# Larger DMA packets on both rings of a sliding-window copy: 32 KB in place of 16 KB

## The chip, the core and the metric

The kernel runs on one core of a Trainium2 chip. The metric is the device time of one execution in microseconds. A profile of one execution is also taken: it records every instruction and every DMA packet.

## What is computed

The input `x` has 32 batches of 4096 rows of 256 float32 numbers. The output holds 127 overlapping windows of 64 rows for each batch, one every 32 rows:

```python
for i in range(n_windows):            # 127
    start = i * stride                # stride 32
    result[:, i] = x[:, start:start + window_size]   # window_size 64
```

Nothing is calculated; it is a copy. Cut each batch into 128 blocks of 32 rows (32 KB each). Window w is block w followed by block w + 1, so every block but the first and the last of a batch is written twice. The input has 134 MB, the output 266 MB.

## The kernel before

The kernel consists of DMAs alone. There are two ways to make the windows, and each has a DMA queue of its own.

**Direct** (queue of SP, `Direct.windows`, line 45; the profile calls this queue q1): the first 21 batches are copied from HBM to HBM. One DMA moves 16 windows of 64 KB. As 127 is not a multiple of 16, the last DMA of a batch moves 15 windows; it is called the *tail* below. This path reads nearly every input block twice.

**Staged** (queue of ACT, `Staged`; q10 in the profile): the last 11 batches go through SBUF. A load (`Staged.load`, line 79) brings 16 blocks, one to each of 16 partitions of a slot. Two stores (`Staged.store`, line 91) write them out, once as the first half of a window and once as the second half. At the edges of a batch a store has 15 blocks. There are 24 slots (`N_TILES` = 6 tiles of four). The order on ACT is written out by hand in `Staged.run`: ten loads ahead (`LEAD`), then in each turn the load of group r + 10 and the two stores of group r. A store waits for the semaphore `loaded` of its slot. A load that reuses a slot waits for the semaphore `stored`, which the two earlier stores raise.

SP and ACT each feed one ring on each of the 16 DMA engines. Each window or block of a DMA goes to one engine. `max_dma_last_dim` sets how long a contiguous piece may be, in bytes, before it is cut. In the kernel before it is 16384 for the full direct DMAs (`DIRECT`) and for loads and stores (`STAGE`), and 32768 for the tail (`2 * DIRECT`). A full direct DMA therefore gives each engine four packets of 16 KB, a tail two packets of 32 KB, and a load or a store two packets of 16 KB. Each DMA ends with a 4-byte packet on every engine that it uses, which raises the semaphore; this is called the completion.

At the end SP waits until the semaphore `done` has counted all direct DMAs and the last stores.

Of the kernel before, what the change touches and what calls it, by code (L numbers as in the profile page):

```python
# [1 line left out]

# [4 lines left out]


DIRECT, STAGE = 16384, 16384
N_STAGED = 11  # L10
N_TILES = 6
LEAD = 10


class Geometry:


    def __init__(self, tc, x, out, B, L, D, W, S, n_win):
        assert W == 2 * S and L % S == 0 and n_win == L // S - 1
        self.x, self.out = x, out  # L20
        self.blk, self.nb, self.nw = S * D, L // S, n_win
        self.done, self.total = tc.alloc_semaphore("done"), 0

    def xap(self, b, block, dims):
        return bass.AP(self.x.tensor, self.x.offset + (b * self.nb + block) * self.blk, dims)

    def oap(self, b, w, half, dims):
        at = ((b * self.nw + w) * 2 + half) * self.blk
        return bass.AP(self.out.tensor, self.out.offset + at, dims)

    def count(self, dma):
        dma.then_inc(self.done, 16)
        self.total += 16


class Direct:


    def __init__(self, g, batches):
        self.g, self.batches = g, batches  # L40

    def windows(self, q, b, w0, n, size):
        g = self.g
        g.count(
            q.dma_start(
                out=g.oap(b, w0, 0, [[2 * g.blk, n], [1, 2 * g.blk]]),
                in_=g.xap(b, w0, [[g.blk, n], [1, 2 * g.blk]]),
                max_dma_last_dim=size,
            )
        )  # L50

    def run(self, q):
        full = self.g.nw // 16 * 16
        for b in self.batches:
            for w0 in range(0, full, 16):
                self.windows(q, b, w0, 16, DIRECT)
            self.windows(q, b, full, self.g.nw - full, 2 * DIRECT)


class Staged:  # L60

    def __init__(self, g, tc, pool, dtype, batches, n_tiles):
        self.g = g
        tiles = [pool.tile([128, g.blk], dtype, name=f"xb{i}") for i in range(n_tiles)]
        self.slots = [t[32 + c : 96 : 4, :] for t in tiles for c in range(4)]
        self.loaded = [tc.alloc_semaphore(f"loaded{i}") for i in range(len(self.slots))]  # L70
        self.stored = [tc.alloc_semaphore(f"stored{i}") for i in range(len(self.slots))]
        self.groups = [(b, j) for b in batches for j in range(0, g.nb, 16)]

    def load(self, q, r):
        g, (b, j) = self.g, self.groups[r]
        n, i = divmod(r, len(self.slots))
        if n:
            q.wait_ge(self.stored[i], 32 * n)
        q.dma_start(
            out=self.slots[i], in_=g.xap(b, j, [[g.blk, 16], [1, g.blk]]),  # L80
            max_dma_last_dim=STAGE,
        ).then_inc(self.loaded[i], 16)

    def store(self, q, r):
        g, (b, j) = self.g, self.groups[r]
        n, i = divmod(r, len(self.slots))
        q.wait_ge(self.loaded[i], 16 * (n + 1))
        for half in (0, 1):
            lo = 1 if half and j == 0 else 0
            hi = 15 if not half and j + 16 == g.nb else 16  # L90
            dma = q.dma_start(
                out=g.oap(b, j + lo - half, half, [[2 * g.blk, hi - lo], [1, g.blk]]),
                in_=self.slots[i][lo:hi, :],
                max_dma_last_dim=STAGE,
            )
            if r + len(self.slots) < len(self.groups):
                dma.then_inc(self.stored[i], 16)
            else:
                g.count(dma)

    def run(self, q, lead):
        for r in range(lead):
            self.load(q, r)
        for r in range(len(self.groups)):
            if r + lead < len(self.groups):
                self.load(q, r + lead)
            self.store(q, r)


@with_exitstack  # L110
def kernel(
    ctx: ExitStack,
    tc: tile.TileContext,
    x: bass.AP,
    window_size: bass.AP,
    stride: bass.AP,
    out: bass.AP,
):
    nc = tc.nc
    W, S = int(window_size), int(stride)  # L120
    B, L, D = x.shape
    n_win = (L - W) // S + 1
    assert out.shape == (B, n_win, W, D)
    g = Geometry(tc, x, out, B, L, D, W, S, n_win)
    pool = ctx.enter_context(tc.tile_pool(name="xb", bufs=1))
    staged = Staged(g, tc, pool, x.dtype, range(B - N_STAGED, B), N_TILES)
    direct = Direct(g, range(B - N_STAGED))
    with tc.tile_critical():
        staged.run(nc.scalar, LEAD)
        direct.run(nc.sync)  # L130
        nc.sync.wait_ge(g.done, g.total)


# [1 line left out]
_INS = ['x', 'window_size', 'stride']  # L135
_OUTS = [((32, 127, 64, 256), 'float32')]

_NUMBERS = {'window_size': 64, 'stride': 32}


# [26 lines left out]
```

## Time and profile before

| | |
|---|---|
| median of 6 runs | 759.18 us (755.99 to 762.4) |
| the profiled execution | 755.99 us; span from its first to its last instruction 754.2 us |
| DMA traffic | 25314 packets, 312.53 MB; 6869 of them are completions |
| direct (q1) | 12705 packets, 174.80 MB, 55.4% of the 16 engines' time |
| staged (q10) | 12606 packets, 137.71 MB, 43.8% |
| DMAs | 147 full direct, 21 tails, 88 loads, 176 stores |

The page gives the DMA engines' share of time in 40 equal slices of the span, as tenths, and below that the GB/s of each slice. The bytes are counted once for each packet. A direct packet costs HBM a read and a write, a load one read, a store one write. The queue lines give packets, MB and the share of the time of the 16 engines that the packets took. The issue lines give the kind of DMA, how many there were, their size, and the median time from issue to landing. A table by time can be asked for any stretch of the span; its last column is again GB/s. A share slightly over 1 arises because a packet's recorded end overlaps the start of the next one by a few nanoseconds.

### The profile page before, as it was taken

What the parts mean: (1) busy time and instruction counts of PE and PEld (TensorE: products, weight loads), DVE (VectorE), ACT (ScalarE), POOL (GpSimd) and SP (SyncE); (2) the same over time, 40 slices, a digit from 0 to 9 for tenths busy, and PEclk for the clock granted to TensorE, in tenths of its full rate; (3) what the DMA queues carried; (4) which work ended last, traced back from release to release, by engine and by line L of the source; (5) the groups of instructions that cost most, each with busy time, mean ns of one, the idle gap of its engine ahead of it and who ended that gap; (6) DMA issues with size and microseconds to landing.
All of it is one profiled execution on the core that took longest, in us unless ns stands there. A gap on an engine that the chain in (4) does not pass through costs nothing. (4 is left out here: it accounts for less than half of the span.)

```text
span 754.2 us, 482 instructions
## 1 busy us (share of the span) xinstructions
POOL 0.2 (0%) x4
## 2 busy tenths in 40 slices
POOL 0000000000000000000000000000000000000000
DMA  8999999999999999999999999999999999999996
GB/s 359 421 403 413 418 424 422 416 423 416 427 418 418 424 420 419 428 415 428 423 425 419 426 421 421 425 418 421 422 423 420 424 419 428 416 424 408 404 403 271
DMA packets 25314, 312.53 MB, mean 414 GB/s; under 512 B 6869, under 2 KB 6869, under 8 KB 6869
## 3 DMA queue, kind: packets, MB, share of 16 engines
q1 hardware_dynamic: 12705, 174.80, 55.4%
q10 hardware_dynamic: 12606, 137.71, 43.8%
q14 instruction: 3, 0.02, 0.0%
HBM read 220.92 MB, written 266.34 MB: 646 GB/s over the span
## 5 line engine op out<-in xcount | busy, mean ns | idle before, releaser
L148 POOL MEMSET const-bfloat16-1.0<- 128x1 bf16 x1 | 0.1, 101 | 0.0
L148 POOL MEMSET const-uint8-127<- 128x1 uint8 x1 | 0.1, 101 | 0.0
L148 POOL MEMSET const-float32-0.0<- 128x1 f32 x1 | 0.1, 98 | 0.2 <-issue 0.2
L148 POOL MEMSET const-float32-1.0<- 128x1 f32 x1 | 0.1, 98 | 0.0
## 6 DMA issues: line engine op xcount, KB each, us to landing
out_dram<-in_x_dram SPq DMA_DIRECT2D x147, 1024.0 KB, 70.0
out_dram<-xb ACTq DMA_DIRECT2D x154, 512.0 KB, 68.8
xb<-in_x_dram ACTq DMA_DIRECT2D x88, 512.0 KB, 71.7
out_dram<-in_x_dram SPq DMA_DIRECT2D x21, 960.0 KB, 69.1
out_dram<-xb ACTq DMA_DIRECT2D x22, 480.0 KB, 69.4
```

The source lines that it names most:

```text
L148: nc = _bacc.Bacc("TRN2", target_bir_lowering=False, num_devices=1)
```

## The change

`DIRECT` and `STAGE` become 32768, and the tail's size becomes `DIRECT`, so that it stays at 32768 bytes:

```diff
-DIRECT, STAGE = 16384, 16384
+DIRECT, STAGE = 32768, 32768
...
-            self.windows(q, b, full, self.g.nw - full, 2 * DIRECT)
+            self.windows(q, b, full, self.g.nw - full, DIRECT)
```

Every data packet of the kernel is then 32 KB: two for each engine in a direct DMA, one in a load or a store. The number of DMAs, their order, their queues, their semaphores and their completions stay as they were.

## The prediction

> **What bounds the kernel now.** No compute engine works here, so I read the DMA lines of the page first: how busy the 16 DMA engines are, what each queue carried, and how long a DMA takes from issue to landing.
>
> ```profile
> span 754.2 us, 482 instructions
> DMA  8999999999999999999999999999999999999996
> GB/s 359 421 403 413 418 424 422 416 423 416 427 418 418 424 420 419 428 415 428 423 425 419 426 421 421 425 418 421 422 423 420 424 419 428 416 424 408 404 403 271
> DMA packets 25314, 312.53 MB, mean 414 GB/s; under 512 B 6869, under 2 KB 6869, under 8 KB 6869
> q1 hardware_dynamic: 12705, 174.80, 55.4%
> q10 hardware_dynamic: 12606, 137.71, 43.8%
> out_dram<-in_x_dram SPq DMA_DIRECT2D x147, 1024.0 KB, 70.0
> out_dram<-xb ACTq DMA_DIRECT2D x154, 512.0 KB, 68.8
> ```
>
> The engines are busy 99.2% of the span (55.4 + 43.8). A DMA lands some 70 us after its issue, so each ring holds tens of microseconds of work in reserve and a late issue costs nothing. The bytes don't change. What can change the time is how fast one engine gets through its packets.
>
> Next, the stretches near the end, as a table by time (columns: length, POOL, clock, DMA share, GB/s):
>
> ```profile
> 100.00:690.00 590.00, 0.00 (x0) 1.00 1.01 421
> 690.00:740.00 50.00, 0.00 (x0) 1.00 0.95 404
> ```
>
> After 690 us the share is 0.95, about 15/16: one engine has finished. The 21 direct tails (15 windows) and 22 of the stores (15 blocks) run on 15 engines. The completion records agree: the 12705 packets of q1 are 147 x 64 + 21 x 30 data packets and 147 x 16 + 21 x 15 completions. So 15 engines set the end. Each carries 588 direct and 528 staged packets of 16 KB, 42 direct ones of 32 KB and 432 completions.
>
> Durations come from the trace's packet records. The usual 16384 B packet lasts 611 ns and the next on its engine starts 607 ns after it; the usual 32768 B packet lasts 1213 ns, period 1209; a completion takes 6 ns of its engine. Hence 602 ns per 16 KB and 5 ns per packet. One engine: 1116 x 607 + 42 x 1209 + 432 x 6 ns = 730.8 us. The first packet starts at 2.4 us of the span and the last ends at about 752, so some 19 us on the slowest engine are neither bytes nor fixed cost. They are **stretch**: packets that last longer than 611 or 1213. Following packets end to start, I find 13 to 21 us of it per engine (about 16) and only 1 to 5 us of gaps. So the stretch is the only thing of size that this change can act on.
>
> From 60 to 682 us the records show:
> - 16 KB direct packets: mean stretch 12.1 ns (12% of them over 15 ns)
> - 16 KB staged packets: 12.2 ns (12%)
> - 32 KB packets (the tails): 51.3 ns (38%)
>
> Two 16 KB packets carry 24.3 ns, one 32 KB packet 51.3. After 682 us it is under 1 ns for every kind.
>
> The table by time shows the same without the records. First four windows in which a tail is moving, then four beside them:
>
> ```profile
> 212.70:221.80 9.10, 0.00 (x0) 1.00 1.01 414
> 353.80:366.00 12.20, 0.00 (x0) 1.00 1.00 412
> 389.70:401.40 11.70, 0.00 (x0) 1.00 1.00 413
> 425.00:437.10 12.10, 0.00 (x0) 1.00 1.00 416
> ...
> 228.00:246.00 18.00, 0.00 (x0) 1.00 1.01 421
> 334.00:352.00 18.00, 0.00 (x0) 1.00 1.01 428
> 369.00:387.00 18.00, 0.00 (x0) 1.00 1.01 430
> 405.00:423.00 18.00, 0.00 (x0) 1.00 1.02 431
> ```
>
> Over all 17 tails between 70 and 650 us the mean is 415 GB/s, over 16 windows beside them 425. The tails already have the packet size that the change gives to all.
>
> [...] and completions count as turns. This is the queue view of the tail window 353.8 to 366:
>
> ```profile
> q1 hardware_dynamic: 192, 2.93, 58.1%
> q10 hardware_dynamic: 192, 2.10, 42.2%
> ```
>
> 192 packets each. [...]
>
> **The change part by part.** The instruction lists differ only in shapes: 16x4x4096 becomes 16x2x8192 for the 147 full direct DMAs, 16x2x4096 becomes 16x8192 for the 88 loads and 176 stores; tails keep 15x2x8192. No DMA, wait or queue order is added or moved.
>
> 1. Fixed cost: an engine's 1116 packets of 16 KB become 558 of 32 KB; 558 x 5 ns = **-2.8 us**, all on the path.
>
> 2. Stretch: the 558 pairs cost 558 x 24.3 = 13.6 us now (average over the loaded part). At the 32 KB rate they cost 558 x 51.3 = 28.6. About 95% lie before the loads end, so **+14 us**. Its bounds are wide. Below: if the tail's stretch belongs to the tail, or to mixing two sizes, it is 0. It may even fall: if stretch goes with the number of descriptors, 1158 data and 432 completions become 600 and 432, and 16 us become 10. Above: 16 KB packets suffer too while 32 KB ones run. Stretch summed over all engines is 259 ns per us with none in flight, 529 with 2 to 4 engines on one, 616 with 4 to 6, 750 with 6 to 8. A line through the ends, carried to 16 engines, gives some 1380, 8.6% of engine time against 2.1% now: +44 us over 670 us. I take the packets' own rate, as 16 engines on 32 KB have not been seen, nor 32 KB on the SBUF side at all.
>
> 3. Turns: per engine before, direct 147 x 5 + 21 x 3 = 798, staged 264 x 3 = 792, so both rings end together. After, direct 168 x 3 = 504, staged 264 x 2 = 528. Direct ends first and 24 staged turns, 12 stores of 1.2 us, run alone for about 15 us. The engines stay full, so I take 0. At the end of the trace a lone direct ring runs at the 607 + 6 ns periods, which supports it. [...]
>
> 4. Waits: an ACT ring that now holds about 25 DMAs of 3 descriptors (68.8 us at 8.3 us per load and two stores) could hold some 37 of 2. But store r waits for load r, issued 10 groups or 30 DMAs earlier, so ACT will wait on `loaded` more. Behind it stand its two stores and the next load; the ring still holds about 20 stores and 9 loads, so this costs 0. Without that cover it would be the load's 70 us latency, once. SP has no such wait.
>
> Sum: -2.8 + 14 + 0 + 0 = +11 us, rounded up to **+12** for the neighbours' stretch in part. Against the profiled execution's own 755.99 (754.2 span and 1.8 around it) that is 768; that execution is the fastest of six, 3.2 below the median of 759.18, so I forecast **771**.
>
> **The rivals.** About 0.5% (3.8 us: 755.4 to 763.0) is what a measurement of this kernel can tell from no change.
> - *Forecast, 32 KB packets stretch more*, 0.66: of it 0.44 near the tails' own rate (764 to 785), 0.22 where neighbours' stretch adds up (785 to 810).
> - *Stretch goes with time, not size*, 0.17: tails stretched because sizes mixed, or because of their windows; uniform 32 KB gives back only the fixed cost, 756.4. Packets still cut at 16 KB on the SBUF side would also land here; the lists speak against it. For it: direct and staged 16 KB packets stretch alike. Against it: the rise with the number of engines on 32 KB.
> - *Stretch goes with descriptors*, 0.17, the other sign: [...] stretch falls from 16 to 10 us or less, and with 2.8 saved the time is 750. It is faster beyond noise once stretch falls by over 1 us. For it: stretch ends at 682 us, near the last issues at 690. Against it: I find no tie between stretch and the moments of issue; and the end of the loads, the last landing at 689, explains the stop as well.
>
> **How the numbers follow.** Likeliest 771; its own range 764 to 800. Leaving out about a tenth at each end, the faster case's lower part and the worst adding-up, gives 752 to 800. Faster 0.17, same 0.17, slower 0.66.
>
> **What would show it.** In the profile after: about 9536 data packets, none of 16384 B; the usual duration still 1213; mean stretch of a 32 KB packet 45 to 60 ns while loads run, near 0 after them; 410 to 416 GB/s in the middle in place of 421; q10 alone at the end. A rate of 424 or more in the middle, or a stretch under 30 ns, makes the forecast wrong. A rate near 421 with a long slow end, q10 under 400 GB/s, would make step 3 the cost.

## The result and the profile after

The changed kernel takes 764.63 us (median of 17 runs) against 759.86 us (38 runs of the kernel before): ratio 1.0062, interval 1.0047 to 1.0077. It is slower, on the side that was forecast, but by 4.8 us in place of 12. That 764.63 lies just inside the low end of the forecast's own range, 764 to 800, is luck: the loss came by another way, as the experiments show.

The profiled execution took 766.59 us. The profile of before is of a run of 755.99 us, the fastest of its kernel, so the two profiles lie 10.6 us apart where the medians lie 4.8, and a difference between these two profiles alone is in part one of single runs. From the page of after: the span, the DMA lines, the queues and the issues.

```profile
span 764.8 us, 482 instructions
DMA  9999999999999999999999999999999999999994
GB/s 368 394 410 411 410 416 413 423 420 420 422 420 417 422 418 418 422 413 413 413 420 430 411 423 416 416 413 418 418 418 418 415 411 423 411 413 415 411 399 178
DMA packets 16408, 312.53 MB, mean 409 GB/s; under 512 B 6869, under 2 KB 6869, under 8 KB 6869
q1 hardware_dynamic: 8001, 174.80, 55.1%
q10 hardware_dynamic: 8404, 137.71, 43.1%
out_dram<-in_x_dram SPq DMA_DIRECT2D x147, 1024.0 KB, 102.9
out_dram<-xb ACTq DMA_DIRECT2D x154, 512.0 KB, 89.1
```

The change did what it says: of 16408 packets of the program 6869 are completions and the other 9536 are data (3 belong to instruction fetch), all of 32768 B. The rings hold more: a DMA lands 89 to 103 us after its issue, in place of some 70. At 168 direct DMAs in some 750 us, or 4.5 us each, the direct ring held about 16 of them before (70.0 us) and about 23 after (102.9 us), as an estimate. The bytes are the same, 312.53 MB, and the engines are nearly as busy as before: 98.2% of the span (55.1 + 43.1) in place of 99.2. The middle of the GB/s row lies a few GB/s lower, and the end is longer.

The table by time shows both differences. The first three rows are of the kernel after, the fourth of the kernel before. Columns: length, POOL, clock, DMA share, GB/s.

```profile
100.00:690.00 590.00, 0.00 (x0) 1.00 1.00 418
690.00:740.00 50.00, 0.00 (x0) 1.00 0.96 410
740.00:765.00 25.00, 0.00 (x0) 1.00 0.53 225
```

```profile
740.00:765.00 25.00, 0.00 (x0) 1.00 0.30 129
```

The reader is to see 418 in place of 421 up to 690 us, and in the last 25 us 5.64 MB still to move (225 GB/s x 25 us) in place of 3.23. The packet records say what is left: direct starts its last packet at 747.0 us, and staged goes on alone to 761.6. In the kernel before the last packets start at 751.2 (direct) and 746.9 (staged). Where it says below that a ring ends, the start of its last packet is meant.

Stretch in the packet records (a packet's time beyond the usual 611 or 1213 ns, from 120 to 600 us, added up for each 32 KB moved) rose from 24.9 to 40.3 ns; direct has 45, staged 34. Summed, an engine has 24.0 us of it in place of 15.8. That is +8.2 us where +14 was forecast, and less the 2.8 us of fixed cost it gives 5.4, about the measured loss. It looked like the forecast mechanism at a smaller size. The experiments show that it is another one.

### The profile page after: what moved, and what is told of

Same layout as the page of the kernel before. It is cut to its first block, busy times and chain, and to the rows that moved or that the text cites. A ratio compares the mean times of both kernels' runs of the same rounds, so it can differ in the third digit from the quotient of the medians.

```text
span 764.8 us, 482 instructions
## 1 busy us (share of the span) xinstructions
POOL 0.2 (0%) x4
## 2 busy tenths in 40 slices
DMA packets 16408, 312.53 MB, mean 409 GB/s; under 512 B 6869, under 2 KB 6869, under 8 KB 6869
## 3 DMA queue, kind: packets, MB, share of 16 engines
q1 hardware_dynamic: 8001, 174.80, 55.1%
q10 hardware_dynamic: 8404, 137.71, 43.1%
HBM read 220.92 MB, written 266.34 MB: 637 GB/s over the span
## 6 DMA issues: line engine op xcount, KB each, us to landing
out_dram<-in_x_dram SPq DMA_DIRECT2D x147, 1024.0 KB, 102.9
```

## The experiments

Four theories:
- **Size** (the forecast's): a 32 KB packet stretches more than two of 16 KB, and disturbs its neighbours.
- **Window**: the tails stretch because of their addresses or their 15 engines.
- **Place** or **time**: in both kernels stretch vanishes in the last 75 to 90 us; this depends on the addresses, or on when it is.
- **Share**, later called the HBM theory: a direct byte is read from HBM and written to it, a staged one touches HBM once (the page's 220.92 MB read are the 174.78 of the direct copies and the 46.14 of the loads, its 266.34 MB written the 174.78 again and the 91.55 of the stores). What counts is which part of the engines' time the direct ring gets, and this follows from the turns. A turn is what an engine takes from one ring before it takes from the other. Here it is one data packet or one completion: wherever the packet records from 120 to 600 us leave only one packet that can be the next on an engine, it belongs to the other ring in 7445 of 7470 cases in the kernel before and in all 4681 in the changed one. A direct DMA takes 5 turns of an engine at 16 KB and 3 at 32 KB, a load or a store 3 and 2. Direct moves 12.8 KB per turn against 10.7 at 16 KB (6 to 5), but 21.3 against 16 at 32 KB (4 to 3).

### One ring alone at 32 KB

The direct ring alone:

```diff
-DIRECT, STAGE = 32768, 32768
+DIRECT, STAGE = 32768, 16384
```

> Only the direct ring at 32 KB; loads and stores stay at 16 KB. Direct then moves 21.3 KB per turn against 10.7 KB, two thirds of the engine time, and ends early; staged runs alone for the last 110 us or so. Size theory: direct packets stretch about 47 ns as in the changed kernel, staged ones about 22 per 16 KB as beside the tails; no stretch once staged is alone; time 762 to 768. Share theory (stretch grows with the direct ring's share of the engines, as each of its bytes costs HBM a read and a write): stretch well above the changed kernel's, 60 ns or more per 32 KB on both rings, time over 768. If a lone staged ring were slower than two rings, the last 110 us would show it: under 400 GB/s.

Measured: 804.18 us, ratio 1.057 (1.0536 to 1.0605). All ratios of this part are against runs of the kernel before that were taken beside the experiment.

The staged ring alone (tails stay at 32 KB):

```diff
-DIRECT, STAGE = 16384, 16384
+DIRECT, STAGE = 16384, 32768
```

> Only the staged ring at 32 KB; full direct DMAs stay at 16 KB, tails at 32 KB. Direct then has 44% of the engine time until staged ends at about 590 us, after that it runs alone. Size theory: staged packets stretch about 33 ns per 32 KB or more as in the changed kernel, direct ones 12 to 20 per 16 KB, until staged ends. Share theory: before 590 us stretch is below that of the kernel before (under 24 ns per 32 KB on both rings), and it rises once direct is alone, with under 400 GB/s there. Time: 760 to 766 by the size theory; by the share theory it depends on the lone direct ring, over 766.

Measured: 786.27 us, ratio 1.0349 (1.0314 to 1.0384). The halves of the change cost over nine and over five times what the whole costs, so it is no sum of two penalties on packets.

The queue view of the stretch 120 to 600 us (packets, MB, share of the engines), first of the kernel before, then of the changed one, then with direct alone at 32 KB, then with staged alone at 32 KB:

```profile
q1 hardware_dynamic: 8212, 112.73, 56.0%
q10 hardware_dynamic: 8205, 89.63, 44.7%
```

```profile
q1 hardware_dynamic: 5247, 114.69, 57.5%
q10 hardware_dynamic: 5249, 86.03, 42.9%
```

```profile
q1 hardware_dynamic: 5784, 126.30, 66.6%
q10 hardware_dynamic: 5796, 63.35, 33.9%
```

```profile
q10 hardware_dynamic: 6775, 110.87, 54.0%
q1 hardware_dynamic: 6870, 94.67, 46.4%
```

In each of the four the two rings take nearly equal numbers of turns, 8212 and 8205 or, furthest apart, 6870 and 6775, whatever the sizes of the packets; only the bytes per turn differ. Now count HBM: twice the MB of q1, once those of q10, over 480 us. That gives 656 GB/s before, 657 after, 658 with direct at 32 KB, and 625 with staged at 32 KB. Three kernels with engine rates of 422, 418 and 395 GB/s have the same HBM rate. In the fourth, with staged alone at 32 KB, the 32 KB staged packets stretch by only 4.6 ns (the direct ones by 7.6 per 32 KB), and the engines run at 428 GB/s. So a ring of 32 KB packets hardly stretched here, where the mix left HBM at 625, below 656. With direct at 32 KB all packets stretch by 112 ns per 32 KB, the 16 KB staged ones (117) as much as the direct ones (110).

After 605 us this fourth kernel has direct alone, with 16 KB packets nearly all. The queue view from 620 to 740 us:

```profile
q1 hardware_dynamic: 2850, 39.32, 99.5%
```

39.32 MB in 120 us is 328 GB/s, or 655 of HBM: the same ceiling, reached with one ring and the other size. It is the sum of reads and writes that is the same, 655 to 658. If two thirds of the staged bytes are stores (an estimate from 88 loads and 176 stores), the writes alone are 359 GB/s before, 351 with direct at 32 KB and 328 here. These counts do not tell HBM itself from the way to it; "HBM" stands for both.

The reverse is the third kernel, with direct at 32 KB, once staged is alone in it. Its queue view from 680 to 760 us:

```profile
q10 hardware_dynamic: 2827, 30.89, 98.4%
```

That is 386 GB/s, and also all that it asks of HBM. Its packets stretch here too, by 106 ns per 32 KB, in another manner: 14% of them are over 15 ns longer than usual, half of these by more than 271 ns; while the rings were mixed 60% of the staged ones were, half of them by more than 88. With HBM far below 656 this stretch has another cause, which stays open.

The losses follow roughly, as estimates from these rates. With staged at 32 KB, 585 us or so at 625 in place of 656 lose 28 us (measured 27). With direct at 32 KB, staged alone for 126 us at 386 loses 52 (measured 45). In the changed kernel 14.6 us of staged alone lose about 6 by the same rate (measured 4.8).

### Tails, and smaller packets

The kernel before with its tails at 16 KB:

```diff
-            self.windows(q, b, full, self.g.nw - full, 2 * DIRECT)
+            self.windows(q, b, full, self.g.nw - full, DIRECT)
```

> The kernel before, with its 21 direct tails cut at 16 KB too. Size theory (a 32 KB packet stretches more than two of 16 KB, and makes its neighbours stretch): stretch in the tail windows falls to that of the rest, about 25 ns per 32 KB moved, and the time falls by some 1 to 3 us (756.5 to 759). Window theory (the tail's windows or its 15 engines are the reason): the tail's packets keep about twice the stretch of the others, about 50 ns per 32 KB, and the time stays within 1 us of before. Turns: direct 840, staged 792 per engine, so direct ends a few us after staged; both theories give this no cost.

Measured: 759.52 us, ratio 1.0004 (0.9987 to 1.0021). Stretch in the middle fell from 24.9 to 17.4 ns, so the windows weren't the reason. But the time didn't fall, and the size theory's gain of 1 to 3 us isn't there. Direct, now with 840 turns, ended at 758.5 us, long after staged (730.7), and alone it stretches, as the lone direct ring above (99.5% of the engines' time for 328 GB/s). These 28 us of one ring alone cost nothing: HBM had 655 GB/s in the middle, and the lone direct ring still kept it at 627 (314 GB/s, twice) from 731 to 745 us.

Both rings at 8 KB, tails at 16 KB:

```diff
-DIRECT, STAGE = 16384, 16384
+DIRECT, STAGE = 8192, 8192
```

> Both rings at 8 KB, tails at 16 KB: the same step in the other direction. Fixed cost of 5 ns for each of some 1160 more packets per engine: +5.8 us. Size theory: stretch per 32 KB moved falls from 24 to about 15 ns, -5 us, so the time is 757 to 763. Share theory: direct's share falls from 54.5% to 52.6% outside the tails, stretch falls by 2 us at most, time 762 to 766. If stretch went with the number of descriptors, it would rise by 10 us or so: 772 or more.

Measured: 762.61 us, ratio 1.003 (1.0016 to 1.0044). The time was allowed by both the size and the share theory. Stretch fell to 10.5 ns per 32 KB (time beyond 309 ns, the usual one of an 8 KB packet), and HBM to 651 GB/s. Unhindered 8 KB packets start 306 ns apart, so 32 KB take an engine at least 1224 ns, against 1214 with 16 KB: its own pace is close to being the limit. That this is the reason for the 651 was not tested. The descriptor rival of the prediction, 772 or more, is out.

### Order and place

Three kernels with the same shapes in other places: direct batches in reverse order (in the changed kernel and in the kernel before), and in the changed kernel batches 0 to 10 staged in place of 21 to 31.

```diff
-    direct = Direct(g, range(B - N_STAGED))
+    direct = Direct(g, range(B - N_STAGED - 1, -1, -1))
```

> The changed kernel with the direct batches in reverse order, 20 down to 0. In both kernels stretch is gone while direct batches 19 and 20 move, the last 75 to 90 us, although loads and issues end at quite different times. Place theory (stretch depends on which addresses the two rings work on together): batches 20 and 19, now first, run with under 5 ns of stretch per packet, or the pattern moves elsewhere, and batches 1 and 0, now last, stretch. Time theory (stretch is a matter of where in the execution one is, e.g. how far engines have drifted apart or how much is queued): the first batches stretch at 60 ns or more and the last two at none, as before, and the time is the same as the changed kernel's, 764 to 765.

> The kernel before with the direct batches in reverse order. Place theory: as in the changed kernel with the order reversed, the stretch moves, and the two reversed kernels differ by the size of packets as the two originals do. Time theory: 759 to 760, stretch of 50 ns per 32 KB in the first 75 us, some 25 in the middle, none in the last 75.

```diff
-    staged = Staged(g, tc, pool, x.dtype, range(B - N_STAGED, B), N_TILES)
-    direct = Direct(g, range(B - N_STAGED))
+    staged = Staged(g, tc, pool, x.dtype, range(N_STAGED), N_TILES)
+    direct = Direct(g, range(N_STAGED, B))
```

> The changed kernel with batches 0 to 10 staged and 11 to 31 direct; before it was 21 to 31 staged. Place theory: the stretch by direct batch is quite another, and the time may move by up to 15 us either way. Time theory: the same curve over time, with no stretch in the last 80 us; 764 to 765.

Measured: 765.30 us (1.0068, 1.0045 to 1.0090), 760.06 us (0.9993, 0.9979 to 1.0008) and 763.86 us (1.0055, 1.0030 to 1.0080). Stretch keeps its course in all three: 57 to 77 ns per 32 KB in the first 75 us, about the old level in the middle (27 in the kernel before, 41 and 42 in the changed one), about 1 after 690 us. So it is time and not place. The reason for the end was not tested by itself, but fits: from 690 to 740 us one engine is done or runs dry (DMA share 0.95 before, 0.96 after) and 15 ask HBM for 628 GB/s before and 635 after (by the same count), below the 656 of the middle.

### Rings brought back into balance

The changed kernel with its tails at 16 KB, 546 turns against 528:

```diff
-            self.windows(q, b, full, self.g.nw - full, DIRECT)
+            self.windows(q, b, full, self.g.nw - full, DIRECT // 2)
```

> The changed kernel with its tails cut at 16 KB: 546 direct turns against 528 staged, so both rings end within some 10 us of each other in place of staged alone for the last 15 us. If the lone staged ring at the end costs something, the time falls by 2 us or more, to 762 or less. If it costs nothing, as the last packets of the changed kernel suggest (1213 ns each, 1215 ns apart with the completion), the time stays within 1.5 us of 764.6. Size theory adds at most 1 us of gain by less stretch in the tail windows.

Measured: 759.12 us, ratio 0.9989 (0.9971 to 1.0007). The whole loss is gone with 21 DMAs of 432 changed. The rings do not end together here: direct ends at 753.0 us and staged at 736.6, so one ring is alone about as long as in the changed kernel, but it is the one that loads HBM twice per byte (656 GB/s from 737 to 745 us), and nothing is lost. It might still be said that smaller tails calmed their neighbours, so two more kernels part size and balance. In the first nearly all packets are 32 KB and the turns are equal, 528 each; the tails stay at 32 KB:

```diff
-        self.g, self.batches = g, batches
+        self.g, self.batches, self.n = g, batches, 0
...
-            for w0 in range(0, full, 16):
-                self.windows(q, b, w0, 16, DIRECT)
-            self.windows(q, b, full, self.g.nw - full, DIRECT)
+            for w0 in range(0, self.g.nw, 16):
+                self.n += 1
+                size = DIRECT // 2 if self.n % 14 == 7 else DIRECT
+                self.windows(q, b, w0, min(16, self.g.nw - w0), size)
```

> The changed kernel with 12 of its 168 direct DMAs (no tail among them) cut at 16 KB, so that each ring has 528 turns per engine and both end together; nearly all packets are 32 KB. HBM theory (the earlier runs put a ceiling of about 656 GB/s on HBM reads and writes together; what counts is how long the rings are mixed so that HBM is full, and the changed kernel loses its last 15 us, staged alone at some 405 GB/s of HBM): 759 to 760.5, the time of the kernel before; stretch about 27 ns per 32 KB in the middle. Size theory: stretch stays at 40 ns or more and the time at 763 to 766.

In the second, which starts from the kernel before, packets stay at 16 KB, but one more direct DMA of each batch goes to 32 KB, so that direct and staged stand 4 to 3 in bytes per turn, as in the changed kernel:

```diff
-                self.windows(q, b, w0, 16, DIRECT)
+                self.windows(q, b, w0, 16, 2 * DIRECT if w0 == 48 else DIRECT)
```

> The kernel before with one more direct DMA of each batch (windows 48 to 63) at 32 KB, two of eight in place of one; all else at 16 KB. Direct then has 756 turns against 792, the same 14.2 to 10.7 KB per turn (4 to 3) as in the changed kernel, and staged has 12 stores left alone at the end. HBM theory: the loss of the changed kernel without its packet size, 763.5 to 766. Size theory: only 21 of 168 direct DMAs more are at 32 KB, 760 to 762.

Measured: 759.79 us for the first, ratio 0.9998 (0.9986 to 1.0010), and 765.56 us for the second, ratio 1.0071 (1.0053 to 1.0089, four runs). The first has the packets of the change without its time, the second its time with only 42 direct DMAs at 32 KB. The table by time of the last 25 us, first of the one with 32 KB packets, then of the one with 16 KB:

```profile
740.00:765.00 25.00, 0.00 (x0) 1.00 0.33 142
```

```profile
740.00:765.00 25.00, 0.00 (x0) 1.00 0.55 232
```

142 lies beside the 129 of before, 232 beside the 225 of the changed kernel. In the second kernel direct ends at 746.1 us and staged at 761.4, as in the changed one (747.0 and 761.6); in the first, at 753.6 and 752.3. Their queues from 120 to 600 us, in the same order:

```profile
q1 hardware_dynamic: 5435, 113.12, 56.1%
q10 hardware_dynamic: 5439, 89.11, 44.4%
```

```profile
q1 hardware_dynamic: 7864, 114.37, 57.5%
q10 hardware_dynamic: 7863, 85.90, 43.2%
```

56.1% is the share of before, 57.5% that of after, and HBM stands at 657 and 656 GB/s. The balanced kernel has 30.4 ns of stretch per 32 KB. With the fixed period of 1209 ns this makes 1239 ns; before, two periods of 607 and 24.9 ns make the same 1239. The fixed cost saved comes back as stretch: the pace is that of HBM, at 657 GB/s in place of 656.

### One more batch staged

If HBM is the limit, fewer HBM bytes should help. With 12 staged batches HBM moves 4.1 MB less and the engines 4.2 MB more. The mix of sizes keeps the turns about equal: 576 each in the first kernel, which starts from the changed one and takes the loop above with 48 of its 160 direct DMAs at 16 KB; 880 to 864 in the second, which starts from the kernel before and has 8 KB tails:

```diff
-N_STAGED = 11
+N_STAGED = 12
...
+                size = DIRECT // 2 if self.n * 3 // 10 > (self.n - 1) * 3 // 10 else DIRECT
...
```

> 32 KB packets, 12 batches staged in place of 11, and 48 of the 160 direct DMAs at 16 KB, so that both rings have 576 turns. HBM moves 483.1 MB in place of 487.3 (736 us at 656 GB/s in place of 743), the engines 316.7 MB in place of 312.5 (one engine 608 x 1209 + 448 x 6 ns = 737.8 us in place of 730.8). HBM theory: both limits come to lie at about the same time, so 752 to 756; stretch under 12 ns per 32 KB in the middle, some 427 GB/s. Size theory: 767 or more, as 1.3% more bytes come on top of the changed kernel's stretch.

```diff
-N_STAGED = 11
+N_STAGED = 12
...
-            self.windows(q, b, full, self.g.nw - full, 2 * DIRECT)
+            self.windows(q, b, full, self.g.nw - full, DIRECT // 2)
```

> The same with 16 KB packets: 12 batches staged, tails at 8 KB, so that direct has 880 turns and staged 864. HBM theory: now the engines are the limit, and there the 5 ns per packet count: one engine needs about 742 us in place of 737.8, so 755 to 760, some 2 to 4 us above the kernel with 12 staged batches and 32 KB packets. Size theory: below that kernel by 8 us or more.

Measured: 759.15 us, ratio 0.9986 (0.9973 to 0.9999), and 759.06 us, ratio 0.9983 (0.9972 to 0.9995). Stretch in the middle fell to 8.4 and 6.8 ns and the engines' rate there rose to 429 and 428 GB/s, as expected. The gain of 4 us or more did not come. The 1.3% more bytes on the engines take most of it. From its records, the 32 KB kernel needs on one engine 737.8 us of fixed periods and 7.9 us of stretch, against 730.8 and 15.8 before: 745.7 against 746.6. The expectation left out that the stretch of the first 75 us stays (53 and 62 ns per 32 KB there). The expected 2 to 4 us between the two sizes isn't seen either. These two are the only versions whose interval lies wholly below 1, by 0.1 to 0.2%, too little to call a better kernel. A fairer deal of the tails over all 16 engines was not tried.

## Why the prediction was wrong

- **What bounds the kernel.** "The only thing of size that this change can act on" is stretch: right as a reading of the packets, but the prediction never asked what holds the packets up. The page had a line for it. Of before and of after:

```profile
HBM read 220.92 MB, written 266.34 MB: 646 GB/s over the span
```

```profile
HBM read 220.92 MB, written 266.34 MB: 637 GB/s over the span
```

646 over the whole span, start and end included, is close under the 655 to 658 at which the mixes richest in direct bytes stopped in these runs. The limit of the mixed stretch was HBM; the engines' 99% share includes packets held up by it.
- **Step 1, fixed cost, -2.8 us.** Right as a count, worth nothing in time: with the turns balanced, about half the packets give 0.9998.
- **Step 2, stretch, +14 us.** This is the step that failed, together with the price of step 3. Of its rise, 8.2 us were there, 45 (direct) and 34 ns (staged) per packet in place of 51. But 51 ns was no property of 32 KB packets: with the rings balanced, 30.4 ns of stretch on nearly all 32 KB packets cost no time. An engine that is in a tail moves 21.3 KB per direct turn against 10.7 per staged one, so direct has two thirds of it, just as in the kernel with direct alone at 32 KB, where every size stretches. By this account the rise with the number of engines on 32 KB was a rise with direct's share. The prediction had it in view, 58.1% against 42.2% in the tail window, and used it only to show that the turns are equal. Its lines give 2.93 + 2.10 MB in 12.2 us: 412 GB/s of the engines, 652 of HBM. A window beside it, 369 to 387, has these lines:

```profile
q1 hardware_dynamic: 319, 4.18, 54.5%
q10 hardware_dynamic: 324, 3.56, 46.8%
```

  That is 430 GB/s of the engines, 662 of HBM. By the packet records of all the prediction's windows, the 17 with a tail have 415 GB/s of the engines and 659 of HBM, the 16 beside them 425 and 656. The engines moved less in the tails; HBM did not.
- **Step 3, turns.** The count was exact: 504 to 528, staged alone for the last 15 us (14.6). Its price of 0 was wrong: "the engines stay full" holds, with 1215 ns from one lone staged packet to the next, but HBM does not stay full: a lone staged ring asks it for 386 GB/s, as the kernel with direct at 32 KB shows. The loss is there, 4.8 us, and three kernels take it out or bring it in with only some of the packet sizes changed: tails at 16 KB (0.9989), balanced turns (0.9998), and 4 to 3 with 16 KB packets (1.0071). The lone direct ring, from which the step argued, loads HBM twice as much per byte and says nothing of a lone staged one. The turns themselves held: the equal counts of the two rings, 8212 and 8205 or 5784 and 5796, fit a turn of one data packet or one completion.
- **Step 4, waits.** Right: ACT waits for `loaded` more (a load and two stores go out within 2 us, at 605.9, 614.5 and 623.9 us), and by the packet records only the engine that is ahead runs dry, by some 6 us for each group from about 660 to 722 us, off the path.
- **Rivals.** "Stretch goes with time, not size" came nearest in the mechanism: uniform 32 KB alone costs nothing, but with balanced rings it gives 759.79, not the 756.4 that it priced. The descriptor rival is out. Its argument, that stretch stops near the last issue, fell too: in the changed kernel issues and loads go on to 720 us, stretch is gone by about 690.
- **Signs announced.** 418 in the middle was outside 410 to 416, the stretch of 40.3 ns outside 45 to 60, and "a long slow end" was there, with 225 GB/s in the last 25 us: the text had named a slow end as the sign of step 3.

## What to carry to other kernels

Where two queues share the DMA engines as here, a packet size is also a weight: an engine took turns between the rings (8212 and 8205 packets from 120 to 600 us), completions counted as turns, and the bytes per turn set each ring's share: 56.0% of the engines for direct at 6 to 5, 57.5% at 4 to 3, 66.6% at 2 to 1. After a change of size count the turns again. Where one kind of transfer loads HBM twice as much per byte as the other, let the rings end together, or the one that loads HBM more end last: staged alone for 15 us cost 4.8 us, direct alone for 16 or 28 us nothing. And when packets last longer than their usual time, add up HBM reads and writes in that stretch before blaming the packets, and compare the sum with the highest that the kernel's own runs reach, here 655 to 658 GB/s. Where it is below that, as with staged alone at 386 GB/s and 106 ns of stretch, the reason is another.

## What was not expected of the hardware

One core's HBM reads and writes together stopped at 655 to 658 GB/s in the kernels where HBM was the limit, with 16 and 32 KB packets, with mixed rings and with the direct ring alone. At that ceiling stretch grew on both rings: 25 ns per 32 KB with direct at 56.0% of the engines, 40 at 57.5%, 112 at 66.6%. From 20 to 75 us it is about twice that of the middle, in the changed kernel (77 ns per 32 KB against 40) and in the one before (57 against 25) alike, though HBM has only 637 and 642 GB/s there. The ceiling, counted this way, does not explain this stretch; why it is there was left open.
